# Feed-forward of a decoder trunk: the ordinary units' order chosen by readiness, transposes held, second-phase products accumulated in banks already in use

## The chip, the cores and the metric

The kernel runs on one core of one Trainium2 chip. The metric is the device time of one execution in microseconds; lower is better. A run is timed three times or more, and the median stands for it.

## The reference

Two decoder layers over x, 256 tokens of width 2048, all float32. Each layer does

```python
h  = rms_norm(x, norm1_g); z = h @ w_in
out_a = chunked_sgu(gelu(z[..., :2048]), ...)      # spatial gating on 16 channel groups
out_b = swa_sink_attention(z[..., 2048:], ...)     # sliding window of 128, sinks, relative bias
x = x + concat(rms_norm(out_a), rms_norm(out_b)) @ w_out
h2 = rms_norm(x, norm2_g)
x = x + (silu(h2 @ w_gate) * (h2 @ w_up)) @ w_down # D_FF = 5632
```

Everything that the change touches is in the last line, the feed-forward.

## The kernel before

**Exact products from three.** Every weight tile of 256 x 512 arrives by DMA as `raw`. `split2` (lines 91 to 102) has the scalar engine cast it to a rounded `wh` and the vector engine subtract to get the rest `wl`; activations are kept as such pairs too. `mm3` (135) then does three matmuls: high by high, high by low, low by high. So each weight tile costs one cast on ACT, one subtraction on DVE and, for both halves of 128 tokens and both halves of the tile, 12 matmuls on TensorE (PE). This is an ordinary unit, `unit` (140).

**Two streams in the feed-forward.** The hidden width of 5632 is cut into 11 blocks of 512. Blocks 2 to 10 (`S_BLOCKS`) make gate and up by a seven-product scheme, `seven` (583): half units of 6 matmuls each (`s_unit`), on combinations of weight tiles that DVE adds up (609, 610, 615) and one that an accumulating DMA makes (617). The first phase of a block is four rounds of five half units into five PSUM banks `m0` to `m4`; in the middle one ACT copy and five DVE adds combine the banks (625 to 634); the second phase is four rounds of two half units into two more banks, `n0` and `n1`, which DVE then adds (647); Silu and the product with up follow (648, 650). This takes fewer matmuls than ordinary units but more of DVE. Blocks 0 and 1 make gate and up by ordinary units (`gate_up`, 670), and the down product of all blocks is ordinary units too (`down`, 685): a group of blocks is accumulated for one of four column blocks `n` after another, and each group ends with two adds into the residual `xres` (700). The accumulators of ordinary units are the two `dacc` banks until the last half unit is issued, after that the five `acc` banks (`seven_done`).

**What sets the order.** A planner, while the program is written out, keeps a `debt` of DVE time less PE time: `vec` adds 1.14 per large DVE operation (0.6 per small one) and `pe` subtracts 0.227 x 0.95 per matmul. After each half unit the ordinary stream `std_stream` (707) is advanced for as long as the debt is positive:

```python
for _ in s_stream():
    while debt[0] > 0.0 and next(other, False):
        pass
```

The ordinary stream follows a list written by hand, `STD_ORDER` (44): gate and up of block 0, down of blocks (0, 2), gate and up of block 1, down of (1, 3, 4), of (5, 6, 7), of (8, 9) and of (10). `down` yields False while a block of its group has not both of its transposed pairs (687, 688), and then no ordinary unit is issued at that point.

**Transposes.** The activations of a finished block are transposed by `act_T` (569): four transposes into `ps_f`, the only bank of its pool, a cast on ACT (573) and a subtraction on DVE (574) into an `aT` tile, of which there are 8. `act_later` (579) puts the two of a block 2 and 3 ticks off; an ordinary unit is one tick, a half unit half a tick. A tile's allocation waits in its engine's queue if all 8 are taken. The tile framework orders instructions on each engine by its own model of readiness, so the order on the chip is near to the written one and not always the same.

Of the kernel before, what the change touches and what calls it, by code (L numbers as in the profile page):

```python
# [12 lines left out]
F32 = mybir.dt.float32  # L13
F32R = mybir.dt.float32r
BF16 = mybir.dt.bfloat16
AF = mybir.ActivationFunctionType
ALU = mybir.AluOpType
# [4 lines left out]
P = 128  # L22
# [13 lines left out]
NB = 512  # L36
# [4 lines left out]
NFF = DFF // NB  # L41
ND = D // NB
S_BLOCKS = (2, 3, 4, 5, 6, 7, 8, 9, 10)
STD_ORDER = (
    ("gu", 0), ("down", (0, 2)), ("gu", 1), ("down", (1, 3, 4)), ("down", (5, 6, 7)), ("down", (8, 9)), ("down", (10,)),
)
VEC = 1.14
VEC_P = 0.6
MM = 0.227
# [16 lines left out]
def trunk(ctx, tc, x, xt, w_in, w_out, w_gate, w_up, w_down, sgu_w, sgu_g, consts,  # L66
          rel_bias, onehot, radd, out):
    nc = tc.nc
# [4 lines left out]
    zp = ctx.enter_context(tc.tile_pool(name="zp", bufs=8))  # L73
# [3 lines left out]
    pa = ctx.enter_context(tc.tile_pool(name="pa", bufs=5, space=PSUM))  # L77
# [29 lines left out]
    def vec(n, cost=VEC):  # L107
        debt[0] += n * cost
# [7 lines left out]
    def later(delay, fn):  # L116
        pending.append((clock[0] + delay, next(serial), fn))
# [14 lines left out]
        pool, tag = ((pm, "sm"), (pd, "dacc"), (pd, "dacc"))[next(turns) % 3]  # L132
        return pool.tile(shape, F32, tag=tag, name=name)

    def mm3(acc, ah, al, wh, wl, first, last):
        nc.tensor.matmul(acc, ah, wh, start=first, stop=False)  # L136
        nc.tensor.matmul(acc, ah, wl, start=False, stop=False)  # L137
        nc.tensor.matmul(acc, al, wh, start=False, stop=last)  # L138

    def unit(src, acts, acc, first, last):  # L140
        raw = raw_load(src, 2 if clock[0] < 4 else 1)
# [87 lines left out]
    pairs1 = []  # L229
    ss1 = [small([P, ND], "ss4") for t in range(NTOK)]  # L230
# [38 lines left out]
    for lay in range(L):  # L269
# [251 lines left out]
        acc = in_block(4)  # L521
# [35 lines left out]
        rstd2 = [finish_rms(ss2[t], D) for t in range(NTOK)]  # L557
# [7 lines left out]
        ss1 = [small([P, ND], "ss4") for t in range(NTOK)]  # L565
        pairs1 = []
        pairs_f = {}

        def act_T(b, c, sg, pairs_f=pairs_f):
            ps = pm.tile([P, 2, SEQ], F32, tag="sm", name="ps_f")  # L570
            transpose_pair([sg[t][:, 2 * c * P : (2 * c + 2) * P] for t in range(NTOK)], ps)
            pair = tp.tile([P, 2, 2, SEQ], F32R, tag="aT", name="aT")
            nc.scalar.copy(pair[:, 0], ps)
            nc.vector.tensor_tensor(pair[:, 1], ps, f(pair[:, 0]), ALU.subtract)
            vec(1, VEC_P)
            pe(2)
            pairs_f.setdefault(b, []).append(pair)

        def act_later(b, sg, act_T=act_T):
            for c in range(2):  # L580
                later(2 + c, lambda c=c: act_T(b, c, sg))

        def seven(b, lay=lay, pairs2=pairs2, ext2=ext2, act_later=act_later):
            bank = [pa.tile([P, NB], F32, tag="acc", name=f"m{i}") for i in range(5)]

            def s_unit(raw, m, i, op, first, last):
                wh, wl = split2(raw)
                for j in range(2):
                    ah, al = (op(2 * i + j, h) for h in range(2))
                    mm3(bank[m], ah, al, wh[:, j, :], wl[:, j, :], first and j == 0, last and j == 1)  # L590
                pe(6)
                tick(0.5)

            def a_op(k, t):
                return lambda p, h: pairs2[p][:, h, k, t * P : (t + 1) * P]

            def e_op(n):
                return lambda p, h: ext2[p][:, h, n, :]

            kept = []  # L600
            for i in range(4):
                b11 = raw_load(w_gate[lay, b, i, 0])
                b12 = raw_load(w_up[lay, b, i, 0])
                b22 = raw_load(w_up[lay, b, i, 1])
                t2 = ap.tile([P, 2, NB], F32, tag="spt", name="t2", bufs=4)
                first, last = i == 0, i == 3
                s_unit(b11, 0, i, a_op(0, 0), first, last)
                yield
                nc.vector.tensor_tensor(b11, b11, b12, ALU.add)  # L609
                nc.vector.tensor_tensor(t2, b11, b22, ALU.add)  # L610
                s_unit(b11, 1, i, e_op(1), first, last)
                vec(1)
                vec(1)
                yield
                nc.vector.tensor_tensor(b12, b12, b22, ALU.add)
                s_unit(t2, 3, i, e_op(2), first, last)
                nc.gpsimd.dma_start(t2, w_gate[lay, b, i, 1], accum_op=ALU.add)  # L617
                vec(1)
                yield
                s_unit(b12, 2, i, e_op(0), first, last)  # L620
                yield
                s_unit(b22, 4, i, e_op(3), first, last)
                yield
                kept.append(t2)
            m1 = zp.tile([P, NB], F32, tag="z", name="m1")
            nc.scalar.copy(m1, bank[0])
            u1 = zp.tile([P, NB], F32, tag="z", name="u1")
            nc.vector.tensor_tensor(u1, bank[3], m1, ALU.add)
            c22 = zp.tile([P, NB], F32, tag="z", name="c22")
            c21 = zp.tile([P, NB], F32, tag="z", name="c21")  # L630
            nc.vector.tensor_tensor(c21, bank[2], u1, ALU.add)
            nc.vector.tensor_tensor(c22, bank[1], c21, ALU.add)
            nc.vector.tensor_tensor(u1, bank[1], u1, ALU.add)
            nc.vector.tensor_tensor(u1, bank[4], u1, ALU.add)
            vec(5, VEC_P)
            yield
            bank = [pa.tile([P, NB], F32, tag="acc", name=f"n{i}") for i in range(2)]
            for i in range(4):
                b21 = raw_load(w_gate[lay, b, i, 1])
                first, last = i == 0, i == 3  # L640
                s_unit(b21, 0, i, a_op(1, 0), first, last)
                yield
                s_unit(kept[i], 1, i, a_op(1, 1), first, last)
                yield
            sg = [m1, c21]
            for t, m in ((0, m1), (1, c21)):
                nc.vector.tensor_tensor(m, bank[t], m, ALU.add)
                nc.scalar.activation(m, m, AF.Silu, scale=rstd2[t])
            for t, c in ((0, u1), (1, c22)):
                nc.vector.scalar_tensor_tensor(sg[t], c, nrstd2[t], sg[t], ALU.mult, ALU.mult)  # L650
            vec(4, VEC_P)
            act_later(b, sg)
            yield

# [15 lines left out]
        def gate_up(b, even=even, act_later=act_later):  # L670
            acc = yield from even(b, w_gate)
            sg = []
            for t in range(NTOK):
                s = zp.tile([P, NB], F32, tag="z", name="sg")
                nc.scalar.activation(s, acc[t], AF.Silu, scale=rstd2[t])
                sg.append(s)
            acc = yield from even(b, w_up)
            for t in range(NTOK):
                nc.vector.scalar_tensor_tensor(
                    sg[t], acc[t], rstd2[t], sg[t], ALU.mult, ALU.mult  # L680
                )
            vec(NTOK, VEC_P)
            act_later(b, sg)

        def down(blocks, final, lay=lay, pairs_f=pairs_f, norm_block=norm_block, ss1=ss1, pairs1=pairs1):
            for n in range(ND):
                while any(len(pairs_f.get(b, [])) < 2 for b in blocks):
                    yield False
                acc = new_acc() if seven_done[0] else new_acc(pd, "dacc")
                for k, b in enumerate(blocks):  # L690
                    for c in range(2):
                        pair = pairs_f[b][c]
                        unit(
                            w_down[lay, b, n, c], [(pair, 0), (pair, 1)], acc,
                            k == 0 and c == 0, k == len(blocks) - 1 and c == 1,
                        )
                        yield True
                for t in range(NTOK):
                    xs = xres[:, t, n * NB : (n + 1) * NB]
                    nc.vector.tensor_tensor(xs, acc[t], xs, ALU.add)  # L700
                    vec(1, VEC_P)
                    if final and lay == L - 1:
                        nc.sync.dma_start(out[t * P : (t + 1) * P, n * NB : (n + 1) * NB], xs)
                if final and lay < L - 1:
                    norm_block(n, ss1, pairs1, lay + 1, C_G1)

        def std_stream(gate_up=gate_up, down=down):
            for k, (kind, what) in enumerate(STD_ORDER):
                if kind == "gu":
                    yield from gate_up(what)  # L710
                else:
                    yield from down(what, k == len(STD_ORDER) - 1)

        other = std_stream()
        debt[0] = 0.0
# [95 lines left out]
```

## Time and profile before

| | |
|---|---|
| median of 3 runs | 1977.56 us |
| lowest, highest | 1976.96, 1980.13 us |
| span of the profiled execution | 1981.0 us |
| instructions | 25159 |
| PE, DVE, ACT busy | 1956.6, 1723.4, 1151.8 us |
| feed-forward of layer 1, of layer 2 | about 295 to 980 us, about 1285 to 1977 us |

The profiled execution's own time is its span, from its first to its last instruction. PE is matmuls, PEld weight loads that overlap them. In a windows row the columns are the stretch, its length, then each engine's busy time with its number of instructions, the granted clock, the DMA engines' busy share and GB/s. In a timeline row they are start, length, engine, line, operation, output<-input, count and, in brackets, the idle time before it and what ended it. In a group's row, after the count, stand busy time, mean length in ns, and the idle time just before with what ended it.

### The profile page before, as it was taken

What the parts mean: (1) busy time and instruction counts of PE and PEld (TensorE: products, weight loads), DVE (VectorE), ACT (ScalarE), POOL (GpSimd) and SP (SyncE); (2) the same over time, 40 slices, a digit from 0 to 9 for tenths busy, and PEclk for the clock granted to TensorE, in tenths of its full rate; (3) what the DMA queues carried; (4) which work ended last, traced back from release to release, by engine and by line L of the source; (5) the groups of instructions that cost most, each with busy time, mean ns of one, the idle gap of its engine ahead of it and who ended that gap; (6) DMA issues with size and microseconds to landing.
All of it is one profiled execution on the core that took longest, in us unless ns stands there. A gap on an engine that the chain in (4) does not pass through costs nothing.

```text
span 1981.0 us, 25159 instructions
## 1 busy us (share of the span) xinstructions
PE 1956.6 (99%) x8894; PEld 1592.8 (80%) x8894; DVE 1723.4 (87%) x1977; ACT 1151.8 (58%) x1463; POOL 127.0 (6%) x137
## 2 busy tenths in 40 slices
PE   9999999999999999999999999999999999999999
PEld 6788888778887888888888788877788878788887
DVE  6777689999999999999767766899999999999996
ACT  6465566665565565665654655665656555656553
POOL 1211001000000000000002100000000000000000
PEclk9999999999999999999999999999999999999999
DMA  8753657668777768768656445586687776687684
GB/s 316 255 167 129 190 167 225 218 209 247 223 231 235 223 213 259 220 220 265 202 190 190 141 152 178 177 253 195 214 251 218 231 246 202 207 272 209 221 268 141
DMA packets 119712, 424.46 MB, mean 214 GB/s; under 512 B 13169, under 2 KB 15345, under 8 KB 119585
## 3 DMA queue, kind: packets, MB, share of 16 engines
q1 hardware_dynamic: 107072, 377.65, 55.0%
q0 software_dynamic: 12512, 45.19, 12.9%
q8 instruction: 70, 1.15, 0.3%
q14 instruction: 58, 0.47, 0.1%
HBM read 420.66 MB, written 4.23 MB: 214 GB/s over the span
## 4 chain that ended last, share of the span: by engine, by line
PE 82%; DVE 8%; DMA 4%; issue 3%; ACT 2%; POOL 1%; ACTq 0%; SPq 0%; DVEq 0%; POOLq 0%
PE acc L136 9%; PE acc L138 9%; PE acc L137 9%; PE dacc L136 8%; PE dacc L137 8%; PE dacc L138 8%; PE m L137 6%; PE m L138 6%; PE m L136 6%; DVE wl L98 4%; PE n L137 3%; PE n L136 3%; PE n L138 3%; DMA raw<-in_w_down_dram 3%; ACT wh L97 2%
## 5 line engine op out<-in xcount | busy, mean ns | idle before, releaser
L97 ACT CAST wh<-raw 128x1024 fp32r<-128x1024 f32 (+1 forms) x778 | 801.0, 1049 | 652.7 <-DVE raw L609 232.8
L98 DVE TENSOR_TENSOR wl<-raw,wh 128x1024 fp32r<-128x1024 f32 (+1 forms) x778 | 927.4, 1217 | 130.1 <-PE acc L137 54.9
L136 PE MATMUL dacc<-wh,aT 128*128 128x512 f32 x608 | 237.1, 392 | 0.6 <-ACT wh L97 0.2
L137 PE MATMUL dacc<-wl,aT 128*128 128x512 f32 x608 | 237.2, 390 | 0.0
L138 PE MATMUL dacc<-wh,aT 128*128 128x512 f32 x608 | 236.8, 390 | 0.0
L137 PE MATMUL m<-wl,ext 128*128 128x512 f32 x576 | 227.6, 395 | 5.1 <-DVE wl L98 5.1
L136 PE MATMUL m<-wh,ext 128*128 128x512 f32 x576 | 226.9, 394 | 4.7 <-ACT wh L97 4.7
L138 PE MATMUL m<-wh,ext 128*128 128x512 f32 x576 | 224.5, 390 | 0.0
L98 DVE TENSOR_TENSOR wl<-t,wh 128x1024 fp32r<-128x1024 f32 x144 | 175.5, 1219 | 16.8 <-issue 8.0
L136 PE MATMUL acc<-wh,hT 128*128 128x512 f32 x448 | 180.3, 404 | 0.7 <-ACT wh L97 0.7
L97 ACT CAST wh<-t 128x1024 fp32r<-128x1024 f32 x144 | 151.4, 1051 | 47.9 <-PE dacc L138 30.7
L137 PE MATMUL acc<-wl,hT 128*128 128x512 f32 x448 | 175.6, 392 | 0.6 <-DVE wl L98 0.6
L138 PE MATMUL acc<-wh,hT 128*128 128x512 f32 x448 | 175.5, 392 | 0.0
L617 POOL DMA_DIRECT2D t<-in_w_gate_dram x72 | 61.4, 852 | 1374.5 <-DVE wl L98 721.0
L136 PE MATMUL acc<-wh,aT 128*128 128x512 f32 x352 | 139.2, 395 | 0.0
L138 PE MATMUL acc<-wh,aT 128*128 128x512 f32 x352 | 137.4, 390 | 0.0
L137 PE MATMUL acc<-wl,aT 128*128 128x512 f32 x352 | 137.2, 390 | 0.0
L136 PEld LDWEIGHTS dacc<-wh,aT 128*128 128x128 f32 x608 | 114.1, 188 | 26.4 <-DVE xres L700 2.3
L137 PEld LDWEIGHTS m<-wl,ext 128*128 128x128 f32 x576 | 108.1, 188 | 32.9 <-DVE wl L98 11.6
L137 PEld LDWEIGHTS dacc<-wl,aT 128*128 128x128 f32 x608 | 114.2, 188 | 24.7 <-DVE wl L98 1.5
L138 PEld LDWEIGHTS dacc<-wh,aT 128*128 128x128 f32 x608 | 114.1, 188 | 23.6
L136 PEld LDWEIGHTS m<-wh,ext 128*128 128x128 f32 x576 | 108.2, 188 | 30.1 <-ACT wh L97 8.0
(150 smaller groups left out, 3040.7 us busy)
## 6 DMA issues: line engine op xcount, KB each, us to landing
raw<-in_w_gate_dram SPq DMA_DIRECT2D x176, 512.0 KB, 5.6
raw<-in_w_up_dram SPq DMA_DIRECT2D x176, 512.0 KB, 4.5
raw<-in_w_down_dram SPq DMA_DIRECT2D x176, 512.0 KB, 5.3
raw<-in_w_in_dram SPq DMA_DIRECT2D x108, 512.0 KB, 4.3
t<-in_w_gate_dram POOLq DMA_DIRECT2D x72, 512.0 KB, 6.4
raw<-in_w_out_dram SPq DMA_DIRECT2D x64, 512.0 KB, 3.7
bias<-rdram POOLq DMA_DIRECT2D x8, 512.0 KB, 4.4
xr<-in_xt_dram SPq DMA_DIRECT2D x8, 256.0 KB, 5.7
```

Of the source, the lines that this page charges most:

```text
L97: nc.scalar.copy(wh[:, j : j + step, :], src)
L98: nc.vector.tensor_tensor(wl[:, j : j + step, :], src, f(wh[:, j : j + step, :]), ALU.subtract)
L136: nc.tensor.matmul(acc, ah, wh, start=first, stop=False)
L137: nc.tensor.matmul(acc, ah, wl, start=False, stop=False)
L138: nc.tensor.matmul(acc, al, wh, start=False, stop=last)
L617: nc.gpsimd.dma_start(t2, w_gate[lay, b, i, 1], accum_op=ALU.add)
```

## The change

- `STD_ORDER` goes. `std_stream` now looks at which blocks are fully transposed: with two or more ready (or all that are left) it takes up to three for `down`; otherwise it takes the next of blocks 0 and 1 for `gate_up`; otherwise it yields False. `down` no longer waits, since its group is ready.
- Transposes that come due are put on the list `held` and issued while fewer than 8 tiles are in use by the planner's count `live`, which falls with the last use of each tile (after the units of the last column block).
- The second phase of `seven` has no banks of its own: `b21` goes on accumulating in bank 0 and `kept` in bank 2. The combining operations are arranged anew for that: five DVE adds in the middle as before, one at the end in place of two, and one of the two Silu reads bank 0 directly. `mm3` gets a switch that turns off a check of the program writer for these two banks.
- In each round of the first phase the half unit of `b22` (bank 4) now comes ahead of that of `b12` (bank 2).

```diff
-STD_ORDER = (
-    ("gu", 0), ("down", (0, 2)), ("gu", 1), ("down", (1, 3, 4)), ("down", (5, 6, 7)), ("down", (8, 9)), ("down", (10,)),
-)
+GU_BLOCKS = tuple(b for b in range(NFF) if b not in S_BLOCKS)
+CHUNK = (2, 3)
+ACT_TILES = 8
...
+        held = []
+        live = [0]
+
+        def release(live=live, held=held, act_T=act_T):
+            while held and live[0] < ACT_TILES:
+                live[0] += 1
+                act_T(*held.pop(0))
+
         def act_later(b, sg, ...):
             for c in range(2):
-                later(2 + c, lambda c=c: act_T(b, c, sg))
+                def ready(c=c):
+                    held.append((b, c, sg))
+                    release()
+
+                later(2 + c, ready)
...
+                s_unit(b22, 4, i, e_op(3), first, last)
+                yield
                 s_unit(b12, 2, i, e_op(0), first, last)
                 yield
-                s_unit(b22, 4, i, e_op(3), first, last)
-                yield
...
-            m1 = zp.tile([P, NB], F32, tag="z", name="m1")
-            nc.scalar.copy(m1, bank[0])
-            u1 = zp.tile([P, NB], F32, tag="z", name="u1")
-            nc.vector.tensor_tensor(u1, bank[3], m1, ALU.add)
...
-            nc.vector.tensor_tensor(c21, bank[2], u1, ALU.add)
+            nc.scalar.copy(m0, bank[0])
+            nc.vector.tensor_tensor(m0, bank[3], m0, ALU.add)
+            nc.vector.tensor_tensor(c12, bank[1], m0, ALU.add)
+            nc.vector.tensor_tensor(c12, bank[4], c12, ALU.add)
+            nc.vector.tensor_tensor(c21, bank[2], m0, ALU.add)
             nc.vector.tensor_tensor(c22, bank[1], c21, ALU.add)
-            nc.vector.tensor_tensor(u1, bank[1], u1, ALU.add)
-            nc.vector.tensor_tensor(u1, bank[4], u1, ALU.add)
             vec(5, VEC_P)
             yield
-            bank = [pa.tile([P, NB], F32, tag="acc", name=f"n{i}") for i in range(2)]
             for i in range(4):
                 b21 = raw_load(w_gate[lay, b, i, 1])
-                s_unit(b21, 0, i, a_op(1, 0), first, last)
+                s_unit(b21, 0, i, a_op(1, 0), False, i == 3)
                 yield
-                s_unit(kept[i], 1, i, a_op(1, 1), first, last)
+                s_unit(kept[i], 2, i, a_op(1, 1), False, i == 3)
                 yield
-            sg = [m1, c21]
-            for t, m in ((0, m1), (1, c21)):
-                nc.vector.tensor_tensor(m, bank[t], m, ALU.add)
-                nc.scalar.activation(m, m, AF.Silu, scale=rstd2[t])
+            nc.vector.tensor_tensor(m0, bank[2], m0, ALU.add)
+            sg = [zp.tile([P, NB], F32, tag="z", name="sg0"), m0]
+            for t, c in ((0, bank[0]), (1, m0)):
+                nc.scalar.activation(sg[t], c, AF.Silu, scale=rstd2[t])
...
-        def down(blocks, final, ...):
+        left = [NFF]
+
+        def down(blocks, ...):
+            left[0] -= len(blocks)
+            final = left[0] == 0
             for n in range(ND):
-                while any(len(pairs_f.get(b, [])) < 2 for b in blocks):
-                    yield False
...
+                        if n == ND - 1:
+                            live[0] -= 1
+                            release()
                         yield True
...
+            gus = list(GU_BLOCKS)
+            downed = set()
+            while left[0]:
+                full = [b for b in sorted(pairs_f) if len(pairs_f[b]) == 2 and b not in downed]
+                rest = left[0] == len(full)
+                if len(full) >= CHUNK[0] or rest:
+                    blocks = full[: CHUNK[1]]
+                    downed.update(blocks)
+                    yield from down(blocks)
+                elif gus:
+                    yield from gate_up(gus.pop(0))
                 else:
-                    yield from down(what, k == len(STD_ORDER) - 1)
+                    yield False
```

More of the change, by code (lines that the diff above doesn't have):

```diff
@@ L133, in small_ps, with mm3 @@
         return pool.tile(shape, F32, tag=tag, name=name)
[L135 to L138, printed above, removed]
+    def mm3(acc, ah, al, wh, wl, first, last, again=False):
+        nc.tensor.matmul(acc, ah, wh, start=first, stop=False, skip_group_check=again)
+        nc.tensor.matmul(acc, ah, wl, start=False, stop=False, skip_group_check=again)
+        nc.tensor.matmul(acc, al, wh, start=False, stop=last, skip_group_check=again)
     def unit(src, acts, acc, first, last):
@@ L577, in act_T, with act_later, s_unit @@
             pairs_f.setdefault(b, []).append(pair)
-        def act_later(b, sg, act_T=act_T):
+        held = []
[4 more added lines that the diff above has]
+                act_T(*held.pop(0))
+        def act_later(b, sg, held=held, release=release):
             for c in range(2):
-                later(2 + c, lambda c=c: act_T(b, c, sg))
+                def ready(c=c):
+                    held.append((b, c, sg))
+                    release()
+                later(2 + c, ready)
         def seven(b, lay=lay, pairs2=pairs2, ext2=ext2, act_later=act_later):
             bank = [pa.tile([P, NB], F32, tag="acc", name=f"m{i}") for i in range(5)]
-            def s_unit(raw, m, i, op, first, last):
+            def s_unit(raw, m, i, op, first, last, bank=bank):
                 wh, wl = split2(raw)
@@ L589, in s_unit @@
                     ah, al = (op(2 * i + j, h) for h in range(2))
-                    mm3(bank[m], ah, al, wh[:, j, :], wl[:, j, :], first and j == 0, last and j == 1)
+                    mm3(
+                        bank[m], ah, al, wh[:, j, :], wl[:, j, :], first and j == 0,
+                        last and j == 1, m in (0, 2),
+                    )
                 pe(6)
@@ L629, in seven @@
-            c22 = zp.tile([P, NB], F32, tag="z", name="c22")
-            c21 = zp.tile([P, NB], F32, tag="z", name="c21")
-            nc.vector.tensor_tensor(c21, bank[2], u1, ALU.add)
+            m0, c12, c21, c22 = (
+                zp.tile([P, NB], F32, tag="z", name=v) for v in ("m0", "c12", "c21", "c22")
+            )
+            nc.scalar.copy(m0, bank[0])
+            nc.vector.tensor_tensor(m0, bank[3], m0, ALU.add)
+            nc.vector.tensor_tensor(c12, bank[1], m0, ALU.add)
+            nc.vector.tensor_tensor(c12, bank[4], c12, ALU.add)
@@ L632, in seven @@
+            nc.vector.tensor_tensor(c21, bank[2], m0, ALU.add)
             nc.vector.tensor_tensor(c22, bank[1], c21, ALU.add)
-            nc.vector.tensor_tensor(u1, bank[1], u1, ALU.add)
-            nc.vector.tensor_tensor(u1, bank[4], u1, ALU.add)
             vec(5, VEC_P)
             yield
-            bank = [pa.tile([P, NB], F32, tag="acc", name=f"n{i}") for i in range(2)]
             for i in range(4):
                 b21 = raw_load(w_gate[lay, b, i, 1])
-                first, last = i == 0, i == 3
-                s_unit(b21, 0, i, a_op(1, 0), first, last)
+                s_unit(b21, 0, i, a_op(1, 0), False, i == 3)
@@ L642, in seven @@
                 yield
-                s_unit(kept[i], 1, i, a_op(1, 1), first, last)
+                s_unit(kept[i], 2, i, a_op(1, 1), False, i == 3)
                 yield
-            sg = [m1, c21]
-            for t, m in ((0, m1), (1, c21)):
-                nc.vector.tensor_tensor(m, bank[t], m, ALU.add)
-                nc.scalar.activation(m, m, AF.Silu, scale=rstd2[t])
-            for t, c in ((0, u1), (1, c22)):
+            nc.vector.tensor_tensor(m0, bank[2], m0, ALU.add)
+            sg = [zp.tile([P, NB], F32, tag="z", name="sg0"), m0]
@@ L650, in seven @@
+            for t, c in ((0, bank[0]), (1, m0)):
+                nc.scalar.activation(sg[t], c, AF.Silu, scale=rstd2[t])
+            for t, c in ((0, c12), (1, c22)):
                 nc.vector.scalar_tensor_tensor(sg[t], c, nrstd2[t], sg[t], ALU.mult, ALU.mult)
-            vec(4, VEC_P)
+            vec(3, VEC_P)
             act_later(b, sg)
@@ L683, in gate_up, with down @@
             act_later(b, sg)
-        def down(blocks, final, lay=lay, pairs_f=pairs_f, norm_block=norm_block, ss1=ss1, pairs1=pairs1):
+        left = [NFF]
+        def down(blocks, lay=lay, pairs_f=pairs_f, norm_block=norm_block, ss1=ss1, pairs1=pairs1, left=left, live=live, release=release):
+            left[0] -= len(blocks)
+            final = left[0] == 0
             for n in range(ND):
-                while any(len(pairs_f.get(b, [])) < 2 for b in blocks):
-                    yield False
                 acc = new_acc() if seven_done[0] else new_acc(pd, "dacc")
@@ L705, in down, with std_stream @@
                     norm_block(n, ss1, pairs1, lay + 1, C_G1)
[L707 to L710, printed above, removed]
+        def std_stream(gate_up=gate_up, down=down, pairs_f=pairs_f, left=left):
+            gus = list(GU_BLOCKS)
[9 more added lines that the diff above has]
+                    yield from gate_up(gus.pop(0))
                 else:
-                    yield from down(what, k == len(STD_ORDER) - 1)
+                    yield False
         other = std_stream()
```

## The prediction

> **What bounds the kernel now.** I read the page first, for the engines' shares and the slices, then the busy time by windows over the two feed-forward phases (the only part that the change touches), then the timeline of TensorE in the windows that stand out, and last the groups and waits that price the edits.
>
> ```profile
> span 1981.0 us, 25159 instructions
> PE 1956.6 (99%) x8894; PEld 1592.8 (80%) x8894; DVE 1723.4 (87%) x1977; ACT 1151.8 (58%) x1463; POOL 127.0 (6%) x137
> PE   9999999999999999999999999999999999999999
> DVE  6777689999999999999767766899999999999996
> PEclk9999999999999999999999999999999999999999
> PE 82%; DVE 8%; DMA 4%; issue 3%; ACT 2%; POOL 1%; ACTq 0%; SPq 0%; DVEq 0%; POOLq 0%
> core 0: us, PE busy (x) PEld busy (x) DVE busy (x) ACT busy (x) POOL busy (x), PEclk, DMA share, GB/s
> 300.00:980.00 680.00, 673.16 (x2988) 550.37 (x2988) 641.59 (x626) 405.97 (x432) 32.24 (x38) 1.00 0.74 229
> 1290.00:1977.00 687.00, 678.88 (x2998) 552.98 (x2996) 639.79 (x622) 399.32 (x421) 29.67 (x35) 1.00 0.72 224
> 840.00:860.00 20.00, 20.00 (x90) 16.57 (x89) 19.60 (x19) 12.03 (x13) 1.70 (x2) 1.00 0.86 249
> ```
>
> TensorE (PE) is the bound nearly everywhere, at full clock. The change adds and removes no matmul, so it can only win back PE's idle time: 680.00 - 673.16 = 6.8 us in the first layer's feed-forward and 687.00 - 678.88 = 8.1 us in the second's, 14.9 us in all. VectorE (DVE) runs at 94% of the same stretches: a stretch in which the planner mixes in too few ordinary units turns DVE-bound. 840:860 is a clean stretch: about 88 matmuls in 20 us, 0.227 us each (two of the 90 hang over the edges).
>
> **Where PE idles.** By the planner's own ledger one half unit adds 1.14 (split) - 6 x 0.227 x 0.95 = -0.15, a DVE add of weights +1.14, an ordinary unit 1.14 - 12 x 0.227 x 0.95 = -1.45, and ordinary units are issued until the debt is no longer positive. Walked with these constants, STD_ORDER runs dry twice a layer: `gate_up(0)` ends, `("down", (0, 2))` needs block 0's two transposes, which are due 2 and 3 ticks later, only half units tick (0.5 each), and so six half units in a row pass with no ordinary unit; the same again after `gate_up(1)`. The walk puts 12 ordinary units per layer behind the last half unit. The trace agrees with that: of the 352 `acc<-wh,aT` matmuls below, 256 are w_out's (2 layers x 32 units x 4), and 96 = 24 units x 4 are these tails.
>
> ```profile
> 403.00:413.00 10.00, 8.25 (x38) 6.10 (x37) 9.94 (x10) 7.63 (x10) 0.86 (x1) 1.00 0.63 184
> 587.00:607.00 20.00, 17.75 (x82) 13.66 (x81) 19.90 (x21) 10.78 (x15) 1.71 (x2) 1.00 0.64 184
> 1387.00:1397.00 10.00, 8.15 (x38) 6.05 (x37) 9.90 (x11) 7.22 (x9) 0.85 (x1) 1.00 0.60 179
> 1571.00:1591.00 20.00, 17.76 (x83) 13.62 (x82) 19.90 (x22) 10.80 (x15) 1.70 (x2) 1.00 0.63 184
> 404.26 0.40 PE L138 MATMUL m<-wh,hT 128*128 128x512 f32 x1
> 404.49 0.60 PE L201 MATMUL ps_f<-ident,sg 128*128 128x128 f32 x4
> 405.31 0.49 PE L136 MATMUL m<-wh,ext 128*128 128x512 f32 x1 [0.22 <-ACT wh L97]
> 406.57 0.50 PE L137 MATMUL m<-wl,ext 128*128 128x512 f32 x1 [0.76 <-DVE wl L98]
> 406.91 0.40 PE L138 MATMUL m<-wh,ext 128*128 128x512 f32 x1
> 408.07 0.60 PE L201 MATMUL ps_f<-ident,sg 128*128 128x128 f32 x4
> 409.44 0.50 PE L136 MATMUL m<-wh,ext 128*128 128x512 f32 x1 [0.77 <-ACT wh L97]
> L136 PE MATMUL acc<-wh,aT 128*128 128x512 f32 x352 | 139.2, 395 | 0.0
> ```
>
> These four windows are the dry stretches (`ps_f<-ident,sg` are the transposes waited for): DVE is busy 99% of each and PE waits for `wh` and `wl`. Their idle time is 1.75 + 2.25 + 1.85 + 2.24 = 8.1 us. That is a lower bound, because a matmul is drawn 0.39 us long while the next may start after 0.227, which hides 0.16 us of every gap. By starts: four transposes take (0.60 - 0.27)/3 = 0.11 us apiece (0.27 is the drawn length of one), so the first window's 30 matmuls and 8 transposes are 30 x 0.227 + 8 x 0.11 = 7.7 us of work in 10, and the four windows (8, 16, 8 and 16 transposes) lose 2.3 + 3.3 + 2.3 + 3.0 = 10.9 us.
>
> The Trainium skill (Perfetto Trace Analysis, section Identifying the Most-Contended Engine) says that matmul busy time is a poor measure because matmuls are pipelined, and asks for the weight loads' busy share instead. Against the clean stretch's 16.57 in 20 us the four windows' 6.10, 13.66, 6.05 and 13.62 give losses of 2.6, 3.5, 2.7 and 3.6, an estimate of 12.4 us by that page; the row's busy time gives 8.1 and the starts agree with the page more than with the busy time. With 12.4 the forecast below would be 1968.9, with 8.1 it would be 1973.2.
>
> **The change part by part.**
>
> *Order by readiness.* Walked the same way, the new stream never runs dry: when `gate_up(0)` ends only block 2 is full, so `gate_up(1)` starts at once, and when that ends blocks 0, 2 and 3 are full and are taken together; then (1, 4, 5), (6, 7, 8) and (9, 10). All four dry stretches go: -10.9 us, and at least -8.1. What is late next is PE itself: the neighbouring stretches (840:860) have it at 100%.
>
> *Longer runs elsewhere.* The walk also shows how often five half units of the first phase follow each other without an ordinary unit: 5 times per layer before, 11 times after, so 12 more in all.
>
> ```profile
> 315.00:326.00 11.00, 10.56 (x46) 8.20 (x45) 10.83 (x11) 6.95 (x7) 0.89 (x1) 1.00 0.83 232
> 1300.00:1310.00 10.00, 9.54 (x41) 7.32 (x40) 9.89 (x10) 6.30 (x7) 0.89 (x1) 1.00 0.84 245
> 625.00:645.00 20.00, 19.90 (x88) 16.11 (x87) 18.27 (x18) 11.59 (x12) 0.86 (x1) 1.00 0.85 261
> 1610.00:1628.00 18.00, 17.59 (x77) 14.01 (x76) 16.56 (x16) 9.93 (x11) 0.85 (x1) 1.00 0.86 248
> 326.00:340.00 14.00, 14.00 (x63) 11.53 (x62) 13.87 (x13) 9.42 (x11) 1.58 (x2) 1.00 0.90 268
> 1485.00:1515.00 30.00, 30.00 (x137) 24.65 (x136) 29.28 (x29) 16.54 (x18) 0.84 (x1) 1.00 0.63 196
> 705.00:715.00 10.00, 9.33 (x43) 7.17 (x42) 9.93 (x11) 6.36 (x8) 0.86 (x1) 1.00 0.90 241
> 1685.00:1700.00 15.00, 13.97 (x60) 10.40 (x59) 14.81 (x15) 9.49 (x11) 0.85 (x1) 1.00 0.91 257
> 709.00:717.00 8.00, 8.00 (x39) 6.59 (x38) 7.41 (x9) 3.68 (x6) 0.19 (x1) 1.00 0.94 250
> 1695.00:1704.00 9.00, 9.00 (x42) 7.38 (x42) 8.34 (x10) 4.60 (x7) 0.29 (x1) 1.00 0.97 292
> 711.72 0.59 ACT L573 CAST aT<-ps_f 128x512 fp32r<-128x512 f32 x1 [2.72 <-PE dacc L138]
> L573 ACT CAST aT<-ps_f 128x512 fp32r<-128x512 f32 x44 | 25.6, 582 | 20.3 <-PE ps_f L201 11.6 <-PE dacc L138 8.7
> L137 PE MATMUL n<-wl,hT 128*128 128x512 f32 x288 | 112.3, 390 | 1.3 <-DVE wl L98 1.3
> L136 PE MATMUL dacc<-wh,aT 128*128 128x512 f32 x608 | 237.1, 392 | 0.6 <-ACT wh L97 0.2
> L647 DVE TENSOR_TENSOR m<-n,m 128x512 f32<-128x512 f32 x18 | 12.3, 683 | 0.0
> L700 DVE TENSOR_TENSOR xres<-dacc,xres 128x512 f32<-128x512 f32 x60 | 39.3, 682 | 0.7 <-PE dacc L138 0.4
> L700 DVE TENSOR_TENSOR xres<-acc,xres 128x512 f32<-128x512 f32 x20 | 13.6, 687 | 14.4 <-PE acc L138 14.4
> L98 DVE TENSOR_TENSOR wl<-raw,wh 128x1024 fp32r<-128x1024 f32 x774 | 924.7, 1219 | 129.6 <-PE acc L137 54.9 <-issue 32.4 <-ACT wh L97 22.2
> ```
>
> Of the ten old runs of five, six lose 0.44, 0.46, 0.10, 0.41, 0.67 and 1.03 us of PE's time (rows of 315:326 to 1610:1628, 705:715 and 1685:1700); in the other four PE has no idle time (326:340 and 1485:1515 are the first and the last of them). Bounds for the 12 new runs: 0, and 12 x 0.85 = 10.2 us (the mean of the last two). I take the old mean, 3.1/10 = 0.31 us each: +3.7 us.
>
> *Fewer DVE operations.* One of the two `L647` adds per block goes (18 x 0.683 = 12.3 us), and with four groups in place of five 16 of the 80 `L700` adds go (10.9 us). On the path this is 0: PE is the bound, and the planner turns the smaller debt into fewer ordinary units among the half units (18 per layer behind the last half unit in place of 12), where PE is the bound too. If the saving did shorten DVE-bound remnants, it could give back at most the 6.8 us of idle outside the four windows.
>
> *Second phase onto used banks.* `b21` adds to bank 0 after the copy `m0`, as the new tile did before. `kept` adds to bank 2, so PE must now wait for `c21`, which reads bank 2 after the last half unit of the first phase (`b12`, now last, writes that bank). Behind a PE that waits there stand all later units, and through their `wh` and `wl` buffers the casts. Cover: one `b21` half unit (6 x 0.227 = 1.36 us) and by the walk two ordinary units (5.4 us), against at most one DVE operation in progress (1.22) and the add (0.68). Bounds: 0, and 18 x 0.7 = 12.6 us if only the half unit covers it. I take 0, the nearest row being that second-phase matmuls waited 1.3 us in all. The swap gives bank 4 the slack that bank 2 loses, and the weight add of `b12` one half unit more: 0.
>
> *Transposes held for a free tile.* Before, the copy into `aT` waits at ACT for the tile 4 times, 8.7 us. By the walk six transposes per layer are now issued directly behind the unit that frees their tile, so 12 such waits of some 2.2 us on ACT, and the `wh` casts queue behind them. In the rows 709:717 and 1695:1704, which hold the old waits, PE is busy 8.00 of 8.00 and 9.00 of 9.00: the casts done ahead cover them. I take 0; without cover it is 12 x 2.2 = 26 us. Holding itself costs no instruction; block 1's two activations stay in their buffers over about one block, and by the walk at most 7 of those 8 buffers are taken.
>
> *The rest.* Silu from the bank in place of the sum, `m0` summed in place, the check switched off and the group opening `dacc` right after `gate_up(1)` (all openings before: 0.6 us of wait over 608 matmuls) are 0.
>
> Sum on the profiled execution: 1981.0 - 10.9 + 3.7 = 1973.8 us. That span is 3.4 us above the median of the three runs, 1977.56, so I carry the difference over: 1977.6 - 7.2 = 1970 us, 0.4% faster.
>
> **The rivals.**
>
> *The gaps only move (no change), 0.17.* The new runs of five cost what the two worst did, 0.85 us each: 1977.6 - 10.9 + 10.2 = 1977 us. For it: DVE is at 94% with little to spare, and the runs of five are where it falls behind outside the dry stretches. Against it: the ten old runs cost 0.31 us on average, and the longest run in the walk's first phases falls from seven half units to five.
>
> *Just-freed tiles stop ACT (slower), 0.15.* The 12 copies that wait for PE at the head of ACT's queue hold up the `wh` casts, and then `wl` and PE. If each wait reaches PE in full: 1977.6 - 10.9 + 3.7 + 26 = 1996 us; it decides from four of the twelve on (8.8 us against 7.2). For it: the 2.72 us wait above is as long as an ordinary unit. Against it: PE had no gap in either place where this happened before.
>
> *All remnants go too (faster, far end).* If fewer DVE operations and no tile waits clear the other idle time as well, 14.9 us scaled by 10.9/8.1 is 20 us: 1957.5 us. It is the low end of the forecast's own case, not a chance beside it.
>
> **How the numbers follow.** Forecast 0.68: faster, 1970 us. About 0.2% (4 us) is what a measurement of this kernel can tell from no change, so the forecast's case counts as faster; the rivals give same 0.17 and slower 0.15. The range reaches down to 1957 and up to 1983: the no-change case whole, and the slower one up to six of its twelve waits (1970 + 13). What lies above 1983 has about 0.1, what lies below 1957 about 0.05.
>
> **What would show it.** Right: no 10 us window of the feed-forward phases, after their first 100 us, with PE under 9.3 us busy; PE's idle time there 8 to 10 us in place of 14.9; `acc<-wh,aT` x384, 64 `L700`-type adds, DVE near 1700 us busy over 1943 instructions, PE instructions unchanged. The second rival is right if the `aT` copies show waits on `dacc` and PE idles on `wh` just behind them; the first if PE has many gaps under 1 us on `wl`. Matmuls into `m` with `hT` that wait for a DVE add would show my zero for the used banks wrong. I am wrong altogether if the four dry stretches have no counterpart missing after, that is, if the walk does not describe the issued order.

## The result and the profile after

| | before | after |
|---|---|---|
| median of 20 runs | 1978.32 us | 1975.36 us |
| lowest to highest | 1975.64 to 1980.84 us | 1972.23 to 1978.06 us |
| ratio, 95% interval | | 0.9984 (0.9977 to 0.9990) |
| span of the first profiled execution | 1981.0 us | 1970.5 us |

The change makes the kernel 0.16% faster, about 3 us, where 0.4% was forecast. The two profiled executions differ by 10.5 us, more than three times as much as the medians. A single execution is one draw from a spread of some 5 us, so below each kernel was profiled a second time and the medians decide.

First, the head of the page after, the four stretches in which TensorE starved before (the second layer's begin 4 us earlier now; columns as before), and the group row that tells how many ordinary units stand behind the last half unit:

```profile
span 1970.5 us, 25079 instructions
PE 1953.7 (99%) x8894; PEld 1591.1 (81%) x8894; DVE 1700.4 (86%) x1943; ACT 1149.0 (58%) x1463; POOL 127.2 (6%) x137
403.00:413.00 10.00, 10.00 (x48) 8.20 (x47) 9.67 (x10) 7.81 (x10) 0.86 (x1) 1.00 0.74 229
587.00:607.00 20.00, 20.00 (x90) 16.57 (x89) 19.86 (x18) 12.74 (x13) 1.03 (x2) 1.00 0.86 287
1383.00:1393.00 10.00, 9.96 (x46) 7.84 (x45) 9.87 (x10) 7.96 (x9) 0.85 (x1) 1.00 0.78 254
1567.00:1587.00 20.00, 20.00 (x90) 16.53 (x90) 19.33 (x17) 12.38 (x13) 0.85 (x1) 1.00 0.88 286
L136 PE MATMUL acc<-wh,aT 128*128 128x512 f32 x384 | 151.9, 395 | 0.0
```

The dry stretches are gone: PE is busy 10.00 of 10.00 where it was 8.25. The other counts are those of the walk too: 384 `acc<-wh,aT` matmuls, 1943 DVE instructions, 1700.4 us of DVE. (Of the 384, 256 are w_out's, and 128 are 16 ordinary units per layer; the other two of the walk's 18 in the tail finish a group that was opened on `dacc`.) So the change did what it says, and yet 3 us came of it. The next rows tell who ended the waits of PE's weight loads in the feed-forward (microseconds in all, times, longest), here of the second profiles, before and then after:

```profile
PEld m L137 <- DVE wl L98: 9.3, 22, 1.2
PEld dacc L137 <- DVE wl L98: 4.2, 12, 0.9
PEld n L137 <- DVE wl L98: 1.8, 2, 1.1
```
```profile
PEld m L137 <- DVE wl L98: 10.7, 17, 1.1
PEld dacc L137 <- DVE wl L98: 8.4, 20, 1.1
```

PE waited 15.3 us for `wl` before (the `n` row is the second phase, which writes `m` after the change) and waits 19.1 us after; in the first profiles it is 17.5 and 14.3, so this sum alone does not rank the two kernels. The four dry stretches held 5.7 of the 15.3 us. They are gone, so the waits after stand elsewhere.

### The profile page after: what moved, and what is told of

It is laid out like the page before. It is cut to its first block, busy times and chain, and to the rows that moved or that the text cites. A ratio compares the mean times of both kernels' runs of the same rounds, so it can differ in the third digit from the quotient of the medians.

```text
span 1970.5 us, 25079 instructions
## 1 busy us (share of the span) xinstructions
PE 1953.7 (99%) x8894; PEld 1591.1 (81%) x8894; DVE 1700.4 (86%) x1943; ACT 1149.0 (58%) x1463; POOL 127.2 (6%) x137
## 4 chain that ended last, share of the span: by engine, by line
PE 85%; DVE 8%; issue 4%; DMA 2%; ACT 1%; POOL 1%; SPq 0%; DVEq 0%; ACTq 0%; POOLq 0%
PE m L137 9%; PE m L138 9%; PE m L136 9%; PE acc L136 9%; PE acc L138 9%; PE acc L137 9%; PE dacc L137 9%; PE dacc L138 8%; PE dacc L136 8%; DVE wl L98 4%; ACT wh L97 1%; PE ps_s L354 1%; PE ps_v L395 1%; PE ps_f L201 1%; DVE raw L624 1%
## 5 line engine op out<-in xcount | busy, mean ns | idle before, releaser
L136 PE MATMUL dacc<-wh,aT 128*128 128x512 f32 x576 | 224.0, 393 | 2.0 <-DVE xres L717 0.9
L137 PE MATMUL dacc<-wl,aT 128*128 128x512 f32 x576 | 225.5, 391 | 0.0
L138 PE MATMUL dacc<-wh,aT 128*128 128x512 f32 x576 | 224.7, 390 | 0.0
L137 PE MATMUL m<-wl,hT 128*128 128x512 f32 x432 | 168.7, 391 | 1.2 <-DVE wl L98 1.1
L136 PE MATMUL m<-wh,hT 128*128 128x512 f32 x432 | 168.2, 390 | 0.5 <-ACT wh L97 0.5
L138 PE MATMUL m<-wh,hT 128*128 128x512 f32 x432 | 168.1, 389 | 0.0
L136 PE MATMUL acc<-wh,aT 128*128 128x512 f32 x384 | 151.9, 395 | 0.0
L138 PE MATMUL acc<-wh,aT 128*128 128x512 f32 x384 | 149.9, 390 | 0.0
L137 PE MATMUL acc<-wl,aT 128*128 128x512 f32 x384 | 149.5, 389 | 0.0
L136 PEld LDWEIGHTS dacc<-wh,aT 128*128 128x128 f32 x576 | 107.9, 188 | 27.3 <-ACT wh L97 2.2
```

The source lines that it names most:

```text
L136: nc.tensor.matmul(acc, ah, wh, start=first, stop=False, skip_group_check=again)
L137: nc.tensor.matmul(acc, ah, wl, start=False, stop=False, skip_group_check=again)
L138: nc.tensor.matmul(acc, al, wh, start=False, stop=last, skip_group_check=again)
```

## The experiments

Each kernel was timed in five rounds against the kernel before on the same chip; ratios are to that kernel, with 95% intervals. "Lost time" below is worked from the trace: the starts of successive matmuls in the two feed-forward phases, less 0.227 us (0.11 us for a transpose), summed over all gaps over 0.07 us. A block end is "covered" here if PE has an ordinary unit between the last half unit of the block and the first of the next.

### The two kernels again

> The kernel before, unchanged, run and profiled once more. Theory S (spread: one profiled execution differs from the median by some us, so that the two profiles' difference of 10.5 us is partly chance): the new profiled span lies nearer to the median, 1976 to 1980 us, against 1981.0 us in the first profile, and the lost time of TensorE in the feed-forward differs from the first profile's. Theory F (the profiles are typical, something outside the profiled span eats the gain): the span is again 1981 us within 0.5 us, the gaps the same. Timed ratio 1.000 by both.

> The changed kernel, unchanged, run and profiled once more. Theory S: the new profiled span is longer than the first one's 1970.5 us, 1972 to 1977 us. Theory F: 1970.5 us within 0.5 us. Timed ratio 0.9984 by both.

Measured 1.0001 (0.9993 to 1.0010) and 0.9985 (0.9973 to 0.9996). The new spans are 1979.1 and 1974.4 us, so theory S holds: of the 10.5 us between the first two profiles more than half was chance. Lost time in the second profiles: 30.2 us before, 27.4 us after. In the four stretches it falls from 12.6 to 1.9 us, about the 10.9 us that the forecast took off; everywhere else it rises from 17.6 to 25.5 us.

### The order alone, and the rest alone

The first kernel takes the readiness order, `held`, `release` and the new `down` and leaves `seven` and `mm3` as they were. The second takes the new `seven` (used banks, its arrangement, the swap) and leaves the streams:

```diff
 order_only:  seven() unchanged, vec(4, VEC_P) at its end; std_stream(), down(), act_later() as in the change
 banks_only:  seven() as in the change, vec(3, VEC_P) at its end; STD_ORDER, down(), act_later() unchanged
```

> The order by readiness and the held transposes alone; the second phase keeps its own two banks, the half units of b12 and b22 stand as before. Theory A (the forecast: the order gives the whole gain, the banks and the swap nothing): ratio 0.9963 if the dry stretches were sized right, or 0.9984 as the whole change if they were sized too large. Theory B (the banks or the swap give back part of it): faster than the whole change, about 0.996, with the two dry stretches a layer gone from the trace and fewer small gaps at the start of each block's first phase than in the whole change.

> The second phase on used banks, the new arrangement of the combining operations and the swap of the half units alone; the ordinary units follow STD_ORDER as before. Theory A: ratio 1.000, the dry stretches still there. Theory B: slower, 1.002, with TensorE waiting where the second phase or the next block's first phase begins. A third possibility: faster by up to 0.998, if the 12 us less of VectorE work shorten the stretches in which VectorE is the bound.

Order alone 0.9925 (0.9911 to 0.9939), the rest alone 1.0033 (1.0022 to 1.0043). The order is worth 15 us, about twice what was forecast for the whole; the rest of the change costs, and theory B holds as far as it goes. Lost time of the order alone: 17.7 us, 12.5 less than before.

### The rest taken apart

> The order by readiness, the held transposes and the swap of the half units of b12 and b22; the second phase keeps its own banks. The order alone ran at 0.9925 of the kernel before, the whole change at 0.9985. Theory B1 (the second phase on used banks gives the gain back): 0.9925. Theory B2 (the swap gives it back): 0.9985. Theory B3 (both, about half each): 0.9955.

> The order by readiness, the held transposes and the second phase on used banks with its arrangement of the combining operations; b12 ahead of b22 as before. Theory B1: 0.9985. Theory B2: 0.9925. Theory B3: 0.9955.

> The second phase on used banks with its arrangement of the combining operations, under STD_ORDER and without the swap. With the swap it ran at 1.0033 of the kernel before. Theory B1: 1.0033 again. Theory B2: 1.000. Theory B3: 1.0015.

> The order by readiness alone, with the limit on tiles in use set so high (99) that no transpose is ever held: each is issued when it is due and waits in the engines' queues for its tile. Theory H1 (holding costs and gains nothing, as the forecast has it): 0.9925, as with holding. Theory H2 (the order without holding stops ACT at the copies): slower, 0.995 or more, with longer waits of the aT copy on dacc than the 1 to 3 us of before.

With the swap 0.9922 (0.9908 to 0.9935): the swap costs nothing in this order. With the used banks 0.9977 (0.9967 to 0.9988): the loss sits there. Used banks under STD_ORDER, without the swap: 1.0011 (1.0002 to 1.0020), short of B1's 1.0033; one and the same edit costs 2 us in the old order and 10 in the new, which a wait on a bank, made in every block, would not explain well. Under STD_ORDER the swap does seem to cost: 1.0033 with it and 1.0011 without, 4 us, by runs on two chips. That is not taken apart here.

Without holding 0.9916 (0.9903 to 0.9930): holding neither costs nor gains. The waits of the copies into `aT`, first without holding and then with it (the order alone in both); the `dacc` rows are the waits for a tile:

```profile
  PE ps_f L201: 10.5, 11
  PE dacc L138: 4.6, 5
```
```profile
  PE ps_f L201: 13.4, 12
  PE dacc L138: 3.3, 2
```

The order of the units on PE gave the hint. Read off the first layer's matmuls (the second layer's are alike), `order_only` and `order_swap` have one or two ordinary units between the last half unit of a block and the first of the next, at every block end; the change, and `order_banks`, have none at seven of eight. The hunk that moves the second phase to used banks also makes one DVE add less per block, and books it: `vec(4, VEC_P)` became `vec(3, VEC_P)`. That is 0.6 of debt less just there, and by the planner's ledger the ordinary unit then comes two half units later.

### The booking

```diff
 full_cost4 (the whole change):        order_cost3 (the order alone):
-            vec(3, VEC_P)             -            vec(4, VEC_P)
+            vec(4, VEC_P)             +            vec(3, VEC_P)
```

Neither adds or takes away an operation. The third kernel is `full_cost4` with `ACT_TILES = 99`.

> The whole change with one number of the planner put back: the end of a block is booked as four small VectorE operations (2.4) as before, in place of three (1.8). No instruction is added or taken away, only the order moves. Theory P (planner: the smaller booking leaves no ordinary unit between the last half unit of a block and the first of the next, where VectorE has two weight adds to make, and PE then waits for wl): ratio near the order alone, 0.9925, with the first half units of a block behind an ordinary unit again. Theory K (banks: PE, ACT or DVE wait on the two banks that are used twice): 0.9985, as the whole change.

> The order alone (own banks, no swap), with the end of a block booked as three small operations although four are made. Theory P: slower than the order alone, 0.998. Theory K: 0.9925, as the order alone.

> The whole change with the booking of four and the limit on tiles set to 99, so that no transpose is held. It has the fewest VectorE operations of all and no waiting list. Theory P: 0.992, as the order without holding, or a little better for 12 us less VectorE work. Theory K: 0.998.

Full change with four booked 0.9915 (0.9902 to 0.9928), order alone with three booked 1.0016 (1.0008 to 1.0025), the third 0.9922 (0.9910 to 0.9934). Theory P holds and theory K falls. One number of the planner is worth 0.70% (14 us) in the full change and 0.9% in the order alone, and with four booked the used banks are worth nothing that can be told (0.9915 against 0.9925). With three booked they are worth something: 0.9977 with them and 1.0016 without, about 8 us in runs on two chips whose intervals lie apart. Order alone with three booked is slower than expected, as slow as if its order had brought nothing: lost time 33.6 us. It makes one DVE add more per block end than the used banks do; that this is the 8 us is likely and not shown.

### The place or the amount

Three booked also leaves fewer ordinary units among the half units everywhere and more for the tail. So the booking was moved inside the block (middle and end; the change has 5 and 3):

```diff
 full_mid3_end5:  vec(3, VEC_P) in the middle, vec(5, VEC_P) at the end     # 8 in all, as the change
 full_mid6_end3:  vec(6, VEC_P) in the middle, vec(3, VEC_P) at the end     # 9 in all, as full_cost4
 full_cost5:      vec(5, VEC_P) in the middle, vec(5, VEC_P) at the end     # 10 in all
```

> The whole change with the booking moved inside a block: three small operations in the middle and five at the end, eight in all as in the change, so that the walk again leaves 18 ordinary units per layer behind the last half unit, but now with an ordinary unit at all nine block ends of a layer (two in the change). Theory PL (the place matters: an ordinary unit must stand between two blocks): 0.992. Theory AM (the amount matters: with eight booked too few ordinary units are mixed in everywhere): 0.9985, as the change.

> The whole change with six booked in the middle and three at the end, nine in all, so that the walk leaves 12 ordinary units per layer behind the last half unit as with four at the end, but has an ordinary unit at only four of nine block ends. Theory AM: 0.9915, as with four at the end. Theory PL: between the change and that, about 0.996.

> The whole change with five booked in the middle and five at the end, ten in all. The walk has an ordinary unit at eight of nine block ends but runs dry in block 10 (six half units at its start), since the ordinary units are used up early. Theory PL: 0.9915 plus one dry stretch a layer of about 3 us, 0.994. Theory AM: a little under 0.9915, less the same dry stretch, 0.993. It shows whether more booking than four goes on helping.

| booked, middle + end | block ends of the first layer with an ordinary unit behind them | ratio |
|---|---|---|
| 5 + 3, the change | 1 of 8 | 0.9985 |
| 6 + 3 | 4 of 8 | 0.9981 (0.9973 to 0.9990) |
| 5 + 4 | 8 of 8 | 0.9915 |
| 3 + 5 | 8 of 8 | 0.9907 (0.9891 to 0.9922) |

The place decides, not the amount: with eight booked as in the change, but an ordinary unit at every block end, the kernel is 18 us under the kernel before, as good as 5 + 4 or a little better (the intervals overlap). With 6 + 3 the gain is hardly better than the change's, less than theory PL expected from four of eight ends. That is a miss of its size, but its trace shows the loss where PL puts it. Counted by whole blocks, from the first half unit of a block to the first of the next, over both layers, the eight blocks that follow an uncovered end lose 15.1 us, and the same eight lose 3.5 us in `full_cost4`, where all ends are covered. The eight that follow a covered end lose 6.7 us in either kernel. In the change the fourteen blocks behind uncovered ends lose 20.4 us against 9.6 in `full_cost4`. By these single profiles an uncovered end costs some 1.4 us in 6 + 3 and 0.8 us in the change; why it costs more in 6 + 3 stays open.

Ten booked ran at 1.0005 (0.9996 to 1.0014), against the expected 0.994. The dry stretch that the walk put into block 10 is there, and larger than sized; here is the first part of it, once per layer:

```profile
875.00:890.00 15.00, 13.32 (x60) 10.04 (x59) 14.31 (x15) 8.01 (x9) 0.85 (x1) 1.00 0.50 142
1860.00:1875.00 15.00, 13.34 (x59) 10.02 (x58) 13.23 (x14) 8.77 (x11) 0.84 (x1) 1.00 0.52 152
```

By starts it loses 4.6 us per layer (2.8 of them in these rows, the rest by 894 us in the first layer), and 1.5 us more per layer go at the end, where PE waits for block 10's transposed `aT` (1.2 us in the first layer): 12 us together, most of the 13 us of lost time (30.4 us) that it has over `full_cost4` (17.4 us).

**What the ordinary unit covers.** DVE at a block end of the change (second profile; start, length, line, output), then PE at the same place:

```profile
861.70 1.22 DVE L625 TENSOR_TENSOR t<-raw 128x1024 f32<-128x1024 f32 x1
862.87 1.23 DVE L98 TENSOR_TENSOR wl<-raw,wh 128x1024 fp32r<-128x1024 f32 x1
864.01 0.68 DVE L657 TENSOR_TENSOR m<-m,m 128x512 f32<-128x512 f32 x1
864.61 0.74 DVE L662 SCALAR_TENSOR_TENSOR sg<-c,nr,sg 128x512 f32<-128x512 f32 x1
865.27 1.22 DVE L98 TENSOR_TENSOR wl<-raw,wh 128x1024 fp32r<-128x1024 f32 x1
866.40 0.75 DVE L662 SCALAR_TENSOR_TENSOR m<-c,nr,m 128x512 f32<-128x512 f32 x1
```
```profile
864.37 0.39 PE L138 MATMUL m<-wh,hT 128*128 128x512 f32 x1
864.60 0.39 PE L136 MATMUL m<-wh,ext 128*128 128x512 f32 x1
865.73 0.39 PE L138 MATMUL m<-wh,ext 128*128 128x512 f32 x1
865.96 0.61 PE L136 MATMUL dacc<-wh,aT 128*128 128x512 f32 x2
866.54 0.50 PE L137 MATMUL dacc<-wl,aT 128*128 128x512 f32 x1
```

PE goes from the block's half units straight into the next block's (`m<-wh,ext` at 864.60) and is through them at 865.96. DVE in that time makes the weight add, the end's add and product; the `wl` that PE needs next starts only at 865.27 and ends at 866.49, and PE's first matmul on it comes at 866.54. PE loses only 0.24 us there at once; more pieces follow, the largest 0.7 us at 879.03, and by 880 us it is 1.5 us. In `full_mid3_end5` the same place:

```profile
854.92 0.74 DVE L662 SCALAR_TENSOR_TENSOR sg<-c,nr,sg 128x512 f32<-128x512 f32 x1
855.59 0.68 DVE L657 TENSOR_TENSOR m<-m,m 128x512 f32<-128x512 f32 x1
856.19 1.21 DVE L625 TENSOR_TENSOR t<-raw 128x1024 f32<-128x1024 f32 x1
857.32 1.22 DVE L98 TENSOR_TENSOR wl<-raw,wh 128x1024 fp32r<-128x1024 f32 x1
```
```profile
854.99 0.39 PE L138 MATMUL m<-wh,hT 128*128 128x512 f32 x1
855.21 0.39 PE L136 MATMUL dacc<-wh,aT 128*128 128x512 f32 x1
857.71 0.39 PE L138 MATMUL dacc<-wh,aT 128*128 128x512 f32 x1
857.93 0.39 PE L136 MATMUL m<-wh,hT 128*128 128x512 f32 x1
```

PE has the 12 matmuls of an ordinary unit from 855.21 to 857.93, on a `wl` made earlier, while DVE makes the end's operations and the add, and there is no gap. Of the change's 19.1 us in which weight loads waited for `wl`, this kernel has left:

```profile
PEld m L137 <- DVE wl L98: 1.5, 3, 1.1
```

Within 12 us behind a block's last Silu the change loses 8.6 us in all its 18 blocks, `full_cost4` 2.9 and `full_mid3_end5` 3.5. (The kernel before loses 7.0 there, though seven of its eight ends are covered, so this count alone does not tell the two cases apart.) The rest of the difference (27.4 us lost in all against 17.4 and 12.9) is spread over the first and second phases. By whole blocks it stands behind the uncovered ends, as counted above. I take it for the lead of DVE, lost at the block end and made up slowly; how the lead shrinks and grows the runs do not show by themselves.

## Why the prediction went wrong, step by step

- **The step that failed is "Fewer DVE operations ... on the path this is 0".** It followed the operation that goes and not the number that tells the planner of it. I had the ledger, saw that the tail grows from 12 to 18 units, and reasoned that PE is the bound in either place. What moved is where ordinary units stand. That step is worth +14 us (0.9985 against 0.9915), outside the bounds that I gave it (0 to a gain). The sum by the runs is -15 (order) - 2 (used banks and swap with four booked) + 14 (booking) = -3 us.
- **Order by readiness, -10.9 us.** Right in kind, and the dry stretches went as the walk had it. The order alone gave 0.9925, -15 us (12 to 18 by its interval). The lost time fell by 12.5 us; the 16 residual adds that go with it are in that number too.
- **Longer runs elsewhere, +3.7 us.** I counted runs of five inside the first phases and priced them by the mean of the old ones. That count was a sign of the smaller booking, not a cost: `full_mid3_end5` has twelve runs of five per layer, the change eleven, and it loses the least time of all. What mattered were the block ends, which I did not count. With 5 + 3 the walk has an ordinary unit at two of nine block ends, before at eight. The count was in my hands and I looked at the other one.
- **The used banks, the swap, the just-freed tiles: 0 each.** Right where the block ends are covered: 0.9915 with the banks against 0.9925 without, 0.9922 with the swap, 0.9916 without holding. In the traces of the change no matmul or weight load into `m` waits for a DVE add, the sign that I had named against the banks. At three booked and under STD_ORDER the two edits do differ from 0, as said above. And the 12 waits of `aT` copies on `dacc` that I counted are one in the change, of 0.5 us (second profile), so the count by the written order did not hold.
- **"It can only win back PE's idle time, 14.9 us" is wrong as a bound.** `full_mid3_end5` won 18 us. The row below is of the change (second profile), then of `full_mid3_end5`, over most of the two feed-forward phases:

```profile
300.00:960.00 660.00, 655.90 (x2912) 535.32 (x2911) 621.73 (x601) 397.32 (x426) 31.81 (x38) 1.00 0.74 231
1290.00:1940.00 650.00, 644.79 (x2852) 524.95 (x2851) 612.41 (x588) 389.21 (x411) 29.67 (x35) 1.00 0.74 230
```
```profile
300.00:960.00 660.00, 657.25 (x2939) 541.05 (x2938) 625.01 (x606) 403.80 (x431) 32.49 (x38) 1.00 0.75 233
1290.00:1940.00 650.00, 648.67 (x2896) 534.72 (x2895) 614.84 (x588) 394.28 (x412) 29.67 (x35) 1.00 0.75 233
```

By busy time the change idles 9.3 us here and the other 4.1: 5.2 us apart. Their medians stand 15 us apart by the two ratios (0.9985 and 0.9907). The weight loads are busy 15.5 us longer in the same stretches (5.73 + 9.77), which at the clean stretch's 16.57 in 20 us is 18.7 us of work. Short gaps hide in the drawn length of a matmul, as I had written for the dry stretches and then forgot for everything else. The rule cited in the prediction from the Trainium skill (Perfetto Trace Analysis, section Identifying the Most-Contended Engine), to go by the weight loads, is borne out by these rows.

The first rival, gaps that only move, came nearest to what happened: the gaps did move, but to the block ends and not into the runs of five where it put them. The counts that I had named as signs of being right (384 matmuls, 64 residual adds, 1943 DVE instructions) all came, and the gain did not: they follow from the edit and say nothing of where the units stand.

## What to carry to other kernels

- When an edit changes a planner's cost as well as an operation, treat the cost as an edit of its own: walk the order with the old number and the new one, and compare what stands at every place where the helper engine (here DVE) has a burst, not only the count that the edit was about.
- An engine that works ahead of the bound one needs cover at the end of each block, where its own serial operations sit; here one ordinary unit of 2.7 us on PE at each of those places was worth 14 us in all, and the version that books 3 + 5 (0.9907) beats both kernels.
- Compare medians, not two profiles, when a few microseconds are asked for, and count lost time by the starts of matmuls or by the weight loads' busy time when the gaps are shorter than a drawn matmul.

## What was new about the hardware

- Two profiled executions of one program differed by 3.9 us in their spans (1970.5 and 1974.4 us) at the same granted clock of 1.00, nearly all of it in the feed-forward of the second layer (690.0 and 693.7 us from its first to the last matmul): equal instructions, in equal order on PE, DVE and ACT, lose different small gaps from one execution to the next.
